# Prompt scores of the second query block: one plain fp32 product, or three fp32r products of high and low parts

## The chip, the cores and the metric

The kernel runs on one core of one Trainium2 chip. The metric is the device time of one execution in microseconds (us), taken as the median of several runs. The engines are named as in the profile: PE is TensorE, DVE is VectorE, ACT is ScalarE, POOL is GpSimd and SP is SyncE, which only issues transfers here. PEld is the weight load of PE.

## The reference, cut to what matters

The program computes one inference step of a decoder with two layers, for one prompt of 256 tokens and 8 sampled tokens: first a gated short convolution, then block-sparse attention with 8 heads of 128. The change lies in the prompt's attention. Since the prompt is exactly one attention block long, each head is plain causal attention over 256 positions:

```
s_own = jnp.einsum('bqhd,bkhd->bhqk', q, k_own, preferred_element_type=jnp.float32) * scale
own_ok = own_pos[None, :] <= q_pos[:, None]
s_own = jnp.where(own_ok[None, None], s_own, -jnp.inf)
...
p = jax.nn.softmax(jnp.concatenate([s_sel, s_own], axis=-1), axis=-1).astype(vs.dtype)
```

All inputs and outputs are fp32.

## The kernel before, in words

The kernel is a pipeline over slabs of weights. A slab is 1024 x 128 of a weight matrix; it is loaded by SP as `raw` (a 128x1024 tile), ACT rounds it into an fp32r tile `hi` (line 124), and DVE subtracts to get the remainder `lo` as another fp32r tile (line 129). The activations are split the same way: `pair[0]` and `pair[1]` each hold a high and a low tile (called m0h, m0l and m1h, m1l in the profile), with 8 rows of columns per partition. A product of fp32 accuracy is then three fp32r matmuls per 128 rows of the contraction: high by high, low by high, high by low (lines 136 to 138). That is 24 matmuls of 264 columns a slab (256 prompt tokens and 8 sampled ones).

Time is cut into slots, one for each slab n, written out by hand: `at(n, phase, f)` hangs a piece of work on slot n, and `begin(n)` runs the pieces phase after phase ("dma", "pe", "s0", "hi", "lo", "s1a", "s1b", "s1", "s1c"). Then come the first 12 matmuls of the slab, the phases "peh" and "s2", and the last 12 matmuls. Each engine works through its own instructions in exactly the order in which this program text issues them. The attention layer begins at slab S = 40. Slabs 47 and on read `pair[1]`, so `pair[0]` is unused from there until the gated attention output is written to it (line 802, from slot 65 on).

For head h the attention work is placed as follows, with n = 56 + h:

- slot n, "pe": `s_mm(h)` (line 646) computes the scores on PE. Query rows 0 to 127 against keys 0 to 127 is line 648, query rows 128 to 255 against all 256 keys is line 649. Both are plain fp32; each is one instruction in the program and two matmul records in the trace.
- slot n, "s0": `s_max(h)` on DVE adds the causal mask (line 657) and takes the two row maxima (659, 660). The slab's `hi` on ACT and `lo` on DVE come next.
- slot n, "s1b": `s_exp(h)` on ACT (line 666), then `s_norm(h)` on DVE (lines 671 to 673).
- slot n + 1, "peh": PE transposes the probabilities (`p_tr`, line 679) and the values (`v_tr`, 638); ACT copies both out in "s2" (683, 642).
- slot n + 2, "pe": the product with the values, `pv(h)` (lines 688, 689), right behind `s_mm(h + 2)`.

Some slots hold extra work on DVE. In slot 56, between its `lo` and `s_norm(0)`, stand the rotation of the sampled keys and their own score (lines 616 to 618 and 725). In slot 57, phase "s1c", stands the rotation of the keys of heads 4 to 7 (`rope`, lines 603 to 606). In slot 58, `d_max` (lines 732, 733) and then `d_norm` (740 to 742) belong to the sampled tokens. Slot 60 begins with a transpose for the sampled tokens (`pd_tr`, lines 749, 750), slot 62 with 32 matmuls of 512 columns (`pvd`, line 768).

Of the kernel before, what the change touches and what calls it, by code (L numbers as in the profile page):

```python
# [10 lines left out]
F32 = mybir.dt.float32  # L11
# [38 lines left out]
def build(tc, a):  # L50
    nc = tc.nc
    pe, act, dve, pool, sp = nc.tensor, nc.scalar, nc.vector, nc.gpsimd, nc.sync

    with ExitStack() as top:
# [13 lines left out]
        def att_tile(nm):  # L68
            return psp.tile([128, 512], F32, tag="att", bufs=3, name=nm)
# [7 lines left out]
        def keep_warm(n):  # L77
            wt = big_tile("warmp")
            for _ in range(n):
# [13 lines left out]
        pair = [[cp.tile([128, NB, ROW], F32R, name=f"m{i}{c}")[:, :, 4:N + 6] for c in "hl"]  # L93
                for i in range(2)]
# [48 lines left out]
        def at(n, phase, f, *args):  # L143
            hooks.setdefault((n, phase), []).append(lambda: f(*args))
# [383 lines left out]
        with tc.tile_pool(name="l1", bufs=1) as p1, ExitStack() as late_pool:  # L528
# [5 lines left out]
            qh = [p1.tile([128, N], F32, name=f"q{h}") for h in range(8)]  # L534
            kall = p1.tile([128, 8 * N], F32, name="kall")
            kh = [kall[:, N * h:N * h + N] for h in range(8)]
# [106 lines left out]

            P_t, PT_t, s_ps, pt_ps, o_ps = {}, {}, {}, {}, {}

            def s_mm(h):
                s = s_ps[h] = att_tile("s")
                pe.matmul(s[:, 0:128], qh[h][:, 0:128], kh[h][:, 0:128], start=True, stop=True)
                pe.matmul(s[:, 128:384], qh[h][:, 128:256], kh[h][:, 0:256], start=True, stop=True)  # L649

            AB = (np.s_[:, 0:128], np.s_[:, 128:384])
            mx_t = {}
# [201 lines left out]

            for h in range(8):
                n = S + 16 + h
                at(n, "pe", s_mm, h)
                at(n, "s0", s_max, h)
                at(n, "s1b", s_exp, h)
                at(n, "s1b", s_norm, h)  # L860
                at(n + 1, "peh", p_tr, h)
                at(n + 1, "peh", v_tr, h)
                at(n + 1, "s2", p_cp, h)
                at(n + 1, "s2", v_cp, h)

                at(n + 2, "s1a", o_cp, h)
# [136 lines left out]
            for i in range(2, 32):  # L1003
                n = S + i
# [11 lines left out]
                h = i % 8  # L1016
# [20 lines left out]
            r = rows[0]  # L1037
# [11 lines left out]
            r = rows[1]  # L1049
# [9 lines left out]
            for k in range(8):  # L1059
                for c in range(2):  # L1060
                    for j in range(4):
                        pe.matmul(ps[32 * j:32 * j + 32], gs[:, c, k, :],  # L1062
                                  wide(raws, k)[:, 256 * j + 128 * c:256 * j + 128 * c + 128],
                                  start=k == 0 and c == 0, stop=k == 7 and c == 1)
# [99 lines left out]
```

## Time and profile before

| what | value |
|---|---|
| median of 3 runs | 280.36 us (280.11 to 280.7) |
| the profiled execution's own time | 280.45 us |
| its span in the trace | 278.7 us |
| mean granted PE clock | 0.996 of full |
| busy: PE, PEld, DVE, ACT, POOL | 272.7, 255.6, 195.6, 155.3, 59.8 us |
| matmuls, moved bytes | 2330, 66.34 MB |

The span runs from the first to the last instruction of the trace; the time around it is 280.45 - 278.7 = 1.75 us. In a line of the trace the first number is the start in us from the start of the span and the second the duration of what is merged in that line; "xN" counts the instructions in it, and a bracket at the end says how long the engine had been idle before and who released it. Matmuls are pipelined: each is shown for some 0.28 us, but the next starts about 0.12 us after it, so that starts are compared, not durations.

### The profile page before, as it was taken

The numbers are of one execution on the slowest core, as the hardware profiler recorded it, in microseconds if no ns is written. First come the engines' busy times: TensorE is split into PE (matmuls) and PEld (weight loads), VectorE is DVE, ScalarE is ACT, GpSimd is POOL, SyncE is SP. The second block draws the span as 40 slices with busy tenths as digits, with TensorE's granted clock in tenths as the row PEclk, the third lists the DMA queues.
The fourth block names the chain that finished last, engine by engine and source line by source line (L and its number), as shares of the span: only waits on it lengthen the run. The fifth ranks groups of instructions, "written<-read, shape, count | busy, mean of one in ns | idle before, by whom it ended". The sixth has DMA issues, their size and how long they took to land.

```text
span 278.7 us, 6245 instructions
## 1 busy us (share of the span) xinstructions
PE 272.7 (98%) x2330; PEld 255.6 (92%) x2330; DVE 195.6 (70%) x377; ACT 155.3 (56%) x294; POOL 59.8 (21%) x130
## 2 busy tenths in 40 slices
PE   8999999999999999999999999999999999999992
PEld 5999999999999999999998997999959987988891
DVE  3868976655766768969999498498626384993745
ACT  4876564444655538557776495567746752571101
POOL 2110532020101102850311158411100030000212
PEclk9999999999999999999999999999999999999998
DMA  7985989999666876134025999999864995781012
GB/s 230 410 266 189 310 274 331 385 373 356 230 211 224 295 238 221 43 119 152 2 75 194 387 399 348 359 335 304 277 223 149 311 379 173 236 290 61 0 78 85
DMA packets 24495, 66.34 MB, mean 238 GB/s; under 512 B 3090, under 2 KB 6930, under 8 KB 24466
## 3 DMA queue, kind: packets, MB, share of 16 engines
q1 hardware_dynamic: 24178, 65.63, 67.4%
q8 instruction: 18, 0.29, 0.4%
q10 hardware_dynamic: 288, 0.33, 0.4%
q14 instruction: 11, 0.09, 0.1%
HBM read 61.55 MB, written 3.35 MB: 233 GB/s over the span
## 4 chain that ended last, share of the span: by engine, by line
PE 98%; DVE 1%; issue 0%
PE acc L136 24%; PE acc L138 24%; PE acc L137 24%; PE c L961 4%; PE sd L716 3%; PE dps L768 3%; PE acc L961 2%; PE acc L465 2%; PE acc L466 2%; PE acc L469 1%; PE so L1062 1%; PE warmp L80 1%; PE s L649 1%; PE o L688 1%; PE c1b L961 1%; PE c1c L961 1%
## 5 line engine op out<-in xcount | busy, mean ns | idle before, releaser
L124 ACT CAST hi<-raw 128x1024 fp32r<-128x1024 f32 x76 | 79.2, 1049 | 35.2 <-DMA raw<-w 22.1
L129 DVE TENSOR_TENSOR lo<-raw,hi 128x1024 fp32r<-128x1024 f32 x76 | 92.7, 1230 | 7.6 <-ACT hi L124 7.4
L138 PE MATMUL acc<-m0h,lo 128*128 128x264 f32 (+1 forms) x280 | 79.4, 284 | 0.0
L137 PE MATMUL acc<-m0l,hi 128*128 128x264 f32 (+1 forms) x280 | 79.3, 283 | 0.0
L136 PE MATMUL acc<-m0h,hi 128*128 128x264 f32 (+1 forms) x280 | 79.3, 283 | 0.0
L136 PE MATMUL acc<-m1h,hi 128*128 128x264 f32 x264 | 76.6, 290 | 0.0
L138 PE MATMUL acc<-m1h,lo 128*128 128x264 f32 x264 | 74.8, 283 | 0.0
L137 PE MATMUL acc<-m1l,hi 128*128 128x264 f32 x264 | 74.7, 283 | 0.0
L136 PEld LDWEIGHTS acc<-m0h,hi 128*128 128x128 f32 x280 | 52.7, 188 | 0.2
L138 PEld LDWEIGHTS acc<-m0h,lo 128*128 128x128 f32 x280 | 52.8, 189 | 0.0
L137 PEld LDWEIGHTS acc<-m0l,hi 128*128 128x128 f32 x280 | 52.7, 188 | 0.0
L136 PEld LDWEIGHTS acc<-m1h,hi 128*128 128x128 f32 x264 | 49.7, 188 | 1.7 <-issue 1.7
L137 PEld LDWEIGHTS acc<-m1l,hi 128*128 128x128 f32 x264 | 49.7, 188 | 0.1
L138 PEld LDWEIGHTS acc<-m1h,lo 128*128 128x128 f32 x264 | 49.7, 188 | 0.0
L421 POOL COPY uo<-up 128x10 f32<-128x10 f32 x8 | 8.0, 1002 | 66.8 <-DVE up L420 58.9
L657 DVE TENSOR_TENSOR s<-s,cst 128x256 f32<-128x256 f32 x8 | 3.4, 430 | 14.7 <-PE s L649 14.7
L799 DVE TENSOR_TENSOR gt<-z,q 128x256 f32<-128x256 f32 x8 | 3.4, 423 | 9.4 <-ACT z L796 9.4
L932 ACT ACTIVATE row<-row,epst 128x1 f32<-128x1 f32 x2 | 0.6, 295 | 16.6 <-DVE row L931 16.6
L666 ACT ACTIVATE P<-s,mx 128x128 f32<-128x128 f32 (+1 forms) x16 | 6.6, 416 | 5.6 <-DVE mx L660 5.6
L796 ACT ACTIVATE z<-acc 128x264 f32<-128x264 f32 x8 | 3.1, 391 | 11.4 <-PE acc L138 11.4
L628 POOL COPY vs<-vh 128x8 f32<-128x8 f32 x8 | 1.6, 204 | 34.9 <-ACT vh L627 34.9
L466 PE MATMUL acc<-m0l,hi 128*128 128x264 f32 x32 | 8.9, 306 | 0.0
(215 smaller groups left out, 415.4 us busy)
## 6 DMA issues: line engine op xcount, KB each, us to landing
raw<-w SPq DMA_DIRECT2D x76, 512.0 KB, 4.7
kv<-kc SPq DMA_DIRECT2D x32, 256.0 KB, 5.7
kv<-vc SPq DMA_DIRECT2D x16, 512.0 KB, 6.6
first<-first SPq DMA_DIRECT2D x6, 388.0 KB, 6.9
k_o<-kall SPq DMA_DIRECT2D x8, 132.0 KB, 5.1
v_o<-vh SPq DMA_DIRECT2D x8, 132.0 KB, 5.2
xf<-kall SPq DMA_DIRECT2D x16, 64.0 KB, 3.1
kall<-gb SPq DMA_DIRECT2D x2, 512.0 KB, 5.0
```

What stands on the lines that cost most here:

```text
L124: act.copy(his[n][sl], raws[n][sl])
L129: dve.tensor_sub(los[n][sl], raws[n][sl], his[n].bitcast(F32)[sl])
L136: pe.matmul(acc, wh, mh[:, k, 0:w], start=first and k == ks[0], stop=False)
L137: pe.matmul(acc, wh, ml[:, k, 0:w], start=False, stop=False)
L138: pe.matmul(acc, wl, mh[:, k, 0:w], start=False, stop=last and k == ks[-1])
L421: pool.tensor_copy(uo[:, f], up[:, T:N + 2])
L465: pe.matmul(accs[s], wh, mh, start=k == 0, stop=False)
L466: pe.matmul(accs[s], wh, ml, start=False, stop=False)
L666: act.activation(P[sl], s_ps[h][sl], AF.Exp, bias=mx[:, 2 + i:3 + i], scale=SCALE, accum_out=mx[:, 4 + i:5 + i])
L716: pe.matmul(s[32 * j:32 * j + 16, 0:256], zq[:, o:o + 16], kt, start=step == 0 and i == 0, stop=step == 3 and i == 3)
L768: pe.matmul(dps[0][32 * j:32 * j + 32, 512 * c:512 * c + 512], pm[b2][pg][:, j, :], kv_tiles[step, j][:, 512 * c:512 * c + 512], start=ste ...
L961: pe.matmul(acc, g[m][:, k, t], wide(d, k)[:, c0:c1], start=k == 0 and i == 0, stop=k == 7 and i == 2)
```

## The change

`s_mm(h)` keeps the first product (query rows 0 to 127) as it is. The second one becomes three fp32r matmuls of 256 columns that accumulate in the same place: query high by key high, query high by key low, query low by key high. A new function `qk_split(h)` makes the parts: ACT casts the 256 key columns and the 128 query columns to fp32r (two instructions), and DVE subtracts each from its fp32 source (two instructions). The parts are kept in `pair[0]`, in the two rows 2 (h mod 4) and the next. `qk_split(h)` hangs on slot 55 + h, phase "s1c": one slot ahead of its `s_mm(h)`, behind everything else that `begin` issues in that slot.

```
+            def qk_part(h, c):
+                r = 2 * (h % 4)
+                return pair[0][c][:, r, 0:256], pair[0][c][:, r + 1, 0:128]
+
+            def qk_split(h):
+                src = kh[h][:, 0:256], qh[h][:, 128:256]
+                for d, x in zip(qk_part(h, 0), src):
+                    act.copy(d, x)
+                for d, x, y in zip(qk_part(h, 1), src, qk_part(h, 0)):
+                    dve.tensor_sub(d, x, y.bitcast(F32))
+
             def s_mm(h):
                 s = s_ps[h] = att_tile("s")
                 pe.matmul(s[:, 0:128], qh[h][:, 0:128], kh[h][:, 0:128], start=True, stop=True)
-                pe.matmul(s[:, 128:384], qh[h][:, 128:256], kh[h][:, 0:256], start=True, stop=True)
+                for i, (c, d) in enumerate(((0, 0), (0, 1), (1, 0))):
+                    pe.matmul(s[:, 128:384], qk_part(h, c)[1], qk_part(h, d)[0], start=i == 0, stop=i == 2)
...
             for h in range(8):
                 n = S + 16 + h
+                at(n - 1, "s1c", qk_split, h)
                 at(n, "pe", s_mm, h)
```

Lines behind this place are numbered 12 to 13 higher in the changed kernel (657 becomes 669, 673 becomes 685). The changed scores are line 661 there, the casts line 653, the subtractions line 655.

The order of DVE in slot 56, from its `lo` to the mask of head 1, is this before:

```order
L129 TENSOR_TENSOR lo_2692<-raw_2486,hi_2643 128x1024
L616 STREAM_SHUFFLE qsr<-ks 32x64
L617 TENSOR_SCALAR ks<-ks,cst 32x64
L618 SCALAR_TENSOR_TENSOR ks<-qsr,cst,ks 32x64
L725 TENSOR_TENSOR pr<-qs,ks 128x4x8 x2
L671 RECIPROCAL mx<-mx 128x2
L673 TENSOR_SCALAR P<-P,mx 128x128
L673 TENSOR_SCALAR P<-P,mx 128x256
L657 TENSOR_TENSOR s<-s,cst 128x2x128
```

and with the change this (m0h and m0l are the two tiles of `pair[0]`):

```order
L129 TENSOR_TENSOR lo_2698<-raw_2486,hi_2643 128x1024
L616 STREAM_SHUFFLE qsr<-ks 32x64
L617 TENSOR_SCALAR ks<-ks,cst 32x64
L618 SCALAR_TENSOR_TENSOR ks<-qsr,cst,ks 32x64
L737 TENSOR_TENSOR pr<-qs,ks 128x4x8 x2
L683 RECIPROCAL mx<-mx 128x2
L685 TENSOR_SCALAR P<-P,mx 128x128
L685 TENSOR_SCALAR P<-P,mx 128x256
L655 TENSOR_TENSOR m0l<-kall,m0h 128x256
L655 TENSOR_TENSOR m0l<-q_1856,m0h 128x128
L669 TENSOR_TENSOR s<-s,cst 128x2x128
```

The two subtractions of head 1 stand behind the normalisation of head 0 and ahead of the mask of head 1.

The order of DVE in slot 57, from the normalisation of head 1 to the mask of head 2, is this before:

```order
L671 RECIPROCAL mx<-mx 128x2
L673 TENSOR_SCALAR P<-P,mx 128x128
L673 TENSOR_SCALAR P<-P,mx 128x256
L603 STREAM_SHUFFLE rsh<-rp 128x264
L604 TENSOR_TENSOR rp<-rp,cst 128x264
L605 TENSOR_TENSOR rsh<-rsh,cst 128x264
L606 TENSOR_TENSOR rp<-rp,rsh 128x264
L657 TENSOR_TENSOR s<-s,cst 128x2x128
```

and with the change this:

```order
L683 RECIPROCAL mx<-mx 128x2
L685 TENSOR_SCALAR P<-P,mx 128x128
L685 TENSOR_SCALAR P<-P,mx 128x256
L603 STREAM_SHUFFLE rsh<-rp 128x264
L604 TENSOR_TENSOR rp<-rp,cst 128x264
L605 TENSOR_TENSOR rsh<-rsh,cst 128x264
L606 TENSOR_TENSOR rp<-rp,rsh 128x264
L655 TENSOR_TENSOR m0l<-kall,m0h 128x256
L655 TENSOR_TENSOR m0l<-q_1857,m0h 128x128
L669 TENSOR_TENSOR s<-s,cst 128x2x128
```

The subtractions of head 2 stand behind the whole rotation.

On PE, the start of slot 57 (scores of head 1, then the slab's matmuls) is this before:

```order
L648 MATMUL s<-kall,q_1856 128x128
L649 MATMUL s<-kall,q_1856 128x256
L136 MATMUL acc<-m1h,hi_2482 128x264
L137 MATMUL acc<-m1l,hi_2482 128x264
L138 MATMUL acc<-m1h,lo_2533 128x264
```

and with the change this:

```order
L659 MATMUL s<-kall,q_1856 128x128
L661 MATMUL s<-m0h 128x256
L661 MATMUL s<-m0l,m0h 128x256
L661 MATMUL s<-m0h,m0l 128x256
L136 MATMUL acc<-m1h,hi_2482 128x264
L137 MATMUL acc<-m1l,hi_2482 128x264
L138 MATMUL acc<-m1h,lo_2533 128x264
```

The second of the three takes the low part of the keys, the third the low part of the queries, and the slab's matmuls stand behind them.

## The prediction

> **What bounds the kernel now.** First the page: its busy line and the chain of work that ended last. Then the list of PE's waits, complete.
>
> ```profile
> PE 272.7 (98%) x2330; PEld 255.6 (92%) x2330; DVE 195.6 (70%) x377; ACT 155.3 (56%) x294; POOL 59.8 (21%) x130
> ...
> PE 98%; DVE 1%; issue 0%
> ```
> ```profile
> PE st L1079 <- DVE row L1076: 1.2, 1, 1.2
> PE warmp L80 <- PEq L1145: 0.8, 1, 0.8
> ```
>
> PE is the path from end to end, and waits only at the very start and the very end, 2.0 us in all. So any PE time saved in the middle shortens the run, and any new wait of PE lengthens it by its full length, because no later slack on PE could absorb it. Two questions decide: what do the products cost on PE, and are the new operands there when PE reaches them?
>
> For the second I read the timeline of PE and of DVE over slots 56 to 61. PE first: the starts of the scores of heads 0 to 5 and of what follows.
>
> ```profile
> 177.51 0.60 PE L649 MATMUL s<-kall,q 128*128 128x256 f32 x2
> ...
> 180.84 0.38 PE L648 MATMUL s<-kall,q 128*128 128x128 f32 x2
> 181.06 0.60 PE L649 MATMUL s<-kall,q 128*128 128x256 f32 x2
> ...
> 181.61 0.28 PE L137 MATMUL acc<-m1l,hi 128*128 128x264 f32 x1
> ...
> 185.07 0.47 PE L648 MATMUL s<-kall,q 128*128 128x128 f32 x2
> 185.37 0.60 PE L649 MATMUL s<-kall,q 128*128 128x256 f32 x2
> 185.81 0.59 PE L688 MATMUL o<-PT,vt 128*128 128x256 f32 x2
> ...
> 189.91 0.38 PE L648 MATMUL s<-kall,q 128*128 128x128 f32 x2
> ...
> 195.32 0.60 PE L649 MATMUL s<-kall,q 128*128 128x256 f32 x2
> ...
> 199.85 0.38 PE L648 MATMUL s<-kall,q 128*128 128x128 f32 x2
> ```
>
> Then DVE in the same stretch.
>
> ```profile
> 178.14 0.43 DVE L657 TENSOR_TENSOR s<-s,cst 128x256 f32<-128x256 f32 x1 [5.01 <-PE s L649]
> ...
> 179.47 1.21 DVE L129 TENSOR_TENSOR lo<-raw,hi 128x1024 fp32r<-128x1024 f32 x1
> ...
> 180.62 0.21 DVE L616 STREAM_SHUFFLE qsr<-ks 32x64 f32<-32x64 f32 x1
> ...
> 181.92 0.55 DVE L673 TENSOR_SCALAR P<-P,mx 128x128 f32<-128x128 f32 x2
> 182.38 0.42 DVE L657 TENSOR_TENSOR s<-s,cst 128x256 f32<-128x256 f32 x1
> ...
> 185.37 0.45 DVE L603 STREAM_SHUFFLE rsh<-rp 128x264 f32<-128x264 f32 x1
> ...
> 187.02 0.42 DVE L657 TENSOR_TENSOR s<-s,cst 128x256 f32<-128x256 f32 x1
> ...
> 190.01 0.42 DVE L732 TENSOR_REDUCE dst<-sd 128x1 f32<-128x257 f32 x1
> 190.46 0.15 DVE L733 TENSOR_SCALAR dst<-dst 128x1 f32<-128x1 f32 x1
> ...
> 196.03 0.43 DVE L657 TENSOR_TENSOR s<-s,cst 128x256 f32<-128x256 f32 x1 [0.91 <-PE s L649]
> ...
> 198.56 0.55 DVE L673 TENSOR_SCALAR P<-P,mx 128x128 f32<-128x128 f32 x2
> ```
>
> What to see: DVE idles 5.01 us ahead of head 0's mask, and then falls behind. PE issues the scores of head 1 at 181.06 and of head 2 at 185.37; DVE masks them only at 182.38 and 187.02. That lag costs nothing today, since PE needs the outcome half a slot later. With the change DVE's work becomes an input of the scores themselves.
>
> **What the change saves on PE.** From line 649 to line 688 behind it lie 185.81 - 185.37 = 0.44 us. In slot 57, line 137 starts at 181.61, one matmul of 0.12 behind line 136, so line 649 held PE for 181.49 - 181.06 = 0.43. The nearest row for an fp32r matmul of 256 columns is the last projection, whose 128x256 matmuls run back to back; here are the first and the 16th of 24.
>
> ```profile
> 263.58 0.28 PE L961 MATMUL c1b<-hi,m0h 128*128 128x256 f32 x1
> ...
> 265.34 0.28 PE L961 MATMUL c1b<-hi,m0h 128*128 128x256 f32 x1
> ```
>
> That is 1.76 / 15 = 0.117 us each, 0.35 for three. Saved are 0.435 - 0.352 = 0.083 us a head, 0.66 us for 8 heads. The Trainium skill (TensorE: Matmul & The Clock Gate, Back-to-back issue gap) gives N / 2.4 + 2.5 ns between warm matmuls, an estimate of 109 ns at 256 columns and so of 0.87 us saved. The row says 117 ns with a weight load for each matmul, and I take the row.
>
> **What it adds on ACT and DVE.** The nearest rows are the same split of the gated output: a cast and a subtraction of 128x256. For 128x128 I take 0.29, a vector instruction of that size.
>
> ```profile
> L802 ACT CAST m0h<-gt 128x256 fp32r<-128x256 f32 x8 | 3.3, 407 | 2.4 <-DVE gt L799 2.4
> ```
> ```profile
> L803 DVE TENSOR_TENSOR m0l<-gt,m0h 128x256 fp32r<-128x256 f32 x8 | 3.2, 401 | 0.0
> ...
> L742 DVE TENSOR_SCALAR dg<-cst,pd 128x128 f32<-128x128 f32 x1 | 0.3, 290 | 0.0
> ```
>
> The next instruction starts some 0.05 before the end of the one ahead (182.38 against 181.92 + 0.55 = 182.47 above), so the low part of the keys is there 0.40 us after DVE turns to it and that of the queries after 0.65. A release from DVE to PE takes 0.06, by the one place where PE waited for DVE (274.21 against 273.75 + 0.40):
>
> ```profile
> 273.75 0.40 DVE L1076 TENSOR_TENSOR row<-g,row 128x48 f32<-128x48 f32 x1
> ```
> ```profile
> 274.21 0.42 PE L1079 MATMUL st<-row,g 128*128 128x48 f32 x2 [1.18 <-DVE row L1076]
> ```
>
> **Are the parts there in time? Slot by slot.** I give the shift of PE against before.
>
> Head 0: ACT ends its `hi` of slot 55 at 175.92, DVE has nothing to do.
>
> ```profile
> 174.87 1.05 ACT L124 CAST hi<-raw 128x1024 fp32r<-128x1024 f32 x1
> ...
> 180.31 0.20 ACT L666 ACTIVATION_READ_ACCUMULATOR P<-s,mx 128x1 f32 x1
> ```
>
> Two casts (0.8 at most) and the subtractions (0.65) end by 177.4, ahead of 177.51: no wait, shift -0.08.
>
> Head 1, slot 57: ACT is through with `s_exp(0)` at 180.51, so its casts are done by 181.3. DVE is not. Up to the end of `s_norm(0)` its order is unchanged, and the subtractions start where head 1's mask started, at 182.38 - 0.08 = 182.30. The queries' low part lands at 182.95, PE can start the third product at 183.01. Without waiting it would have started it at 180.98 (181.06 - 0.08) + 2 x 0.117 = 181.21. **Wait 1.80 us.** Behind it in PE's queue stand all 24 matmuls of slab 57, which need none of this. Shift: -0.08 + 1.80 - 0.08 = +1.64.
>
> Head 2, slot 58: the mask of head 1 can start 0.31 after the third product's start (its 0.28 and a release): 183.32 instead of 182.38. From there to the end of `rope` DVE runs without a gap: 187.02 - 182.38 = 4.64 us. Subtractions from 187.96, third product at 187.96 + 0.65 + 0.06 = 188.67. PE would be ready for it at 185.37 + 1.64 + 0.23 (the first two products) = 187.24. **Wait 1.43 us.** Behind it stand `pv(0)` and slab 58. Shift: 1.64 + 1.43 - 0.08 = +2.99.
>
> Head 3, slot 59: mask of head 2 at 188.98; up to `d_max` 190.01 - 187.02 = 2.99, `d_max` 0.60, subtractions 0.65: 193.22, release 193.28. PE would be ready at 189.91 + 2.99 + 0.22 (line 648's product, 181.06 - 180.84) + 0.23 = 193.35. No wait, with 0.07 to spare.
>
> Heads 4 to 7: the extra work on DVE is over and `pv` fills PE. From mask to the end of `s_norm` DVE takes 3.0 (196.03 to 199.02, `d_max` excluded), so from one third product to the readiness of the next 0.31 + 3.0 + 0.71 = 4.0. PE takes from one to the next 199.85 - 195.32 + 0.22 = 4.75, less the 0.08 saved. Some 0.6 us to spare; slot 62's matmuls add more.
>
> **The sum** against the profiled execution's 280.45: + 1.80 + 1.43 - 0.66 = +2.57, so 283.0 us. That execution lies 0.09 over the median of 280.36, which changes nothing.
>
> One cost the trace hardly shows: the third product's stationary operand is the part waited for, so its weight load cannot run ahead. Line 1079 is such a case, with no gap to be seen; a whole load of 0.19 us is the upper bound.
>
> ```profile
> L136 PEld LDWEIGHTS acc<-m1h,hi 128*128 128x128 f32 x264 | 49.7, 188 | 1.7 <-issue 1.7
> ```
>
> I take 0; twice 0.19 would give 283.4. A gain is excluded, since a load can't end before its data.
>
> **Rivals.**
> - *The parts come in time.* PE then keeps its pace and only the saving is left: 280.45 - 0.66 = 279.8, faster. For it: DVE is 70% busy, and idle 5.01 us just ahead. It decides if the subtractions of head 1 land by 181.15, which is 1.8 us earlier than I find; the order puts 2.9 us of `lo`, key rotation and `s_norm` (179.47 to 182.38) ahead of them, and these durations hardly vary. Chance 6%.
> - *Every later slot waits too.* Head 3 has 0.07 us to spare, heads 4, 5 and 7 some 0.6. If DVE or ACT lose 0.4 more a slot, by the casts that now stand ahead of the copies of lines 683 and 642 on ACT, then slots 57 to 59 grow by 0.4 each: 284.2. Chance 12%.
> - *The clock falls.* The granted clock is 1.00 through a PE wait of 1.18 us, but fell some 1.8 us after the last matmul:
>
> ```profile
> 272.90:274.20 1.30, 0.14 (x8) 0.00 (x0) 1.03 (x4) 0.00 (x0) 1.11 (x2) 1.00 0.54 202
> 274.20:276.40 2.20, 0.42 (x2) 0.30 (x2) 1.57 (x5) 0.29 (x1) 0.00 (x0) 1.00 0.32 119
> 276.40:277.00 0.60, 0.00 (x0) 0.00 (x0) 0.00 (x0) 0.00 (x0) 0.00 (x0) 0.53 0.24 74
> ```
>
>   PE had been busy 0.56 of the 3.5 us before that; beside my waits it is busy over half of any such stretch, which speaks against it. At the start of the run a matmul took 5.63 - 5.42 = 0.21 instead of 0.12:
>
> ```profile
> 5.42 0.42 PE L466 MATMUL acc<-m0l,hi 128*128 128x264 f32 x1
> 5.63 0.42 PE L465 MATMUL acc<-m0h,hi 128*128 128x264 f32 x1
> ```
>
>   A stretch of 3.5 us at that pace loses 1.5 us, so 284.5 for one fall. The Trainium skill (TensorE: Matmul & The Clock Gate, The HAM clock gate) has the clock halve only after an idle window of about 3.4 us; by that rule waits of 1.8 and 1.4 us leave it alone, and the 1.18 us wait agrees. Chance 5%.
> - *Only the first wait is real.* 280.45 + 1.80 - 0.66 = 281.6. The second falls away only if DVE makes up the rotation's 1.65 us (185.37 to 187.02). Chance 4%.
>
> **How the numbers follow.** My forecast keeps 73%: 283.0. From 281.4 (only one wait, and that a little shorter) to 284.7 (every slot, or one fall of the clock) all but the first rival is covered, as are the bounds of the weight load. A difference under 0.2%, 0.56 us, is about what a measurement of this kernel cannot tell from none. Only the first rival is faster, and by 0.66 us barely over that: faster 5%, within 0.2% 3%, slower 92%.
>
> **What would show it.** In the changed profile PE's waits list gets two entries of the new score products behind DVE's subtractions, about 1.8 and 1.4 us, in slots 57 and 58; none in 56 and from 60 on. The three products take 0.35 us where nothing waits, and the slab's matmuls keep 0.12. DVE's mask of head 1 starts near 183.3. The granted clock stays at 1.00. I am wrong if PE waits nowhere, if the waits recur in every slot, or if PE makes up the lost time behind slot 59.

## The result and the profile after

The changed kernel takes 283.37 us, the kernel before 280.24 us beside it (medians of six runs each). One of the six runs of the changed kernel took 731.17 us; without it the median is 283.28 us, and the ratio leaves it out. The ratio is 1.0105, with a 95% interval of 1.0086 to 1.0125: slower by about 3 us (2.4 to 3.5), where 283.0 us was forecast. The profiled execution took 283.79 us, with a span of 282.0 us and a mean granted clock of 0.995.

The busy line and the chain of the changed kernel's page:

```profile
PE 273.2 (97%) x2338; PEld 255.4 (91%) x2338; DVE 201.1 (71%) x393; ACT 158.6 (56%) x310; POOL 61.7 (22%) x130
...
PE 92%; DVE 4%; DMA 2%; ACT 0%; issue 0%; SPq 0%
```

PE's busy time has hardly moved, but DVE now holds 4% of the chain. The chain also follows DVE's own work back from a wait, so its 4% is more than the waits alone. (Busy times of pipelined matmuls overlap, so the saving on PE can't be read from them.) The first row of the list of PE's waits names the place; the columns are the total, the number of waits and the longest:

```profile
PE s L661 <- DVE m0l L655: 2.6, 2, 1.4
```

Line 661 is the three products, line 655 DVE's subtractions: two waits that were not there before. The rows behind it are at the start and the end of the run, as before; one of them, 0.2 us at 8.73 us from the start, is not in the list of the kernel before, and lies ahead of everything compared below. The timeline of PE shows where the two are, with the scores of heads 0 to 3 (slots 56 to 59) and the second block of value products of the sampled tokens as a mark behind the change:

```profile
177.54 0.38 PE L659 MATMUL s<-kall,q 128*128 128x128 f32 x2
...
181.01 0.38 PE L659 MATMUL s<-kall,q 128*128 128x128 f32 x2
181.31 0.39 PE L661 MATMUL s<-m0h 128*128 128x256 f32 x1
183.10 0.38 PE L661 MATMUL s<-m0l,m0h 128*128 128x256 f32 x1 [1.40 <-DVE m0l L655]
183.32 0.36 PE L661 MATMUL s<-m0h,m0l 128*128 128x256 f32 x1
183.52 0.28 PE L136 MATMUL acc<-m1h,hi 128*128 128x264 f32 x1
...
187.10 0.47 PE L659 MATMUL s<-kall,q 128*128 128x128 f32 x2
187.33 0.36 PE L661 MATMUL s<-m0h 128*128 128x256 f32 x1
188.85 0.39 PE L661 MATMUL s<-m0l,m0h 128*128 128x256 f32 x1 [1.16 <-DVE m0l L655]
189.25 0.39 PE L661 MATMUL s<-m0h,m0l 128*128 128x256 f32 x1
189.48 0.59 PE L700 MATMUL o<-PT,vt 128*128 128x256 f32 x2
...
193.60 0.38 PE L659 MATMUL s<-kall,q 128*128 128x128 f32 x2
193.74 0.36 PE L661 MATMUL s<-m0h 128*128 128x256 f32 x1
...
194.18 0.60 PE L700 MATMUL o<-PT,vt 128*128 128x256 f32 x2
...
231.93 3.64 PE L780 MATMUL dps<-kv,pm 128*32 128x512 f32 x32
```

And three of these places in the kernel before: the first score product, the product with the values in slot 59, and the mark behind the change.

```profile
177.29 0.38 PE L648 MATMUL s<-kall,q 128*128 128x128 f32 x2
...
190.56 0.59 PE L688 MATMUL o<-PT,vt 128*128 128x256 f32 x2
...
228.60 3.64 PE L768 MATMUL dps<-kv,pm 128*32 128x512 f32 x32
```

From the first score product to that last mark are 51.31 us before and 54.39 us after: +3.08 us. I call this the stretch below. It is steadier than the span, since runs differ by some tenths before they come to slot 56 at all (177.29 and 177.54 here).

Head 3 waits for nothing: its scores take 194.18 - 193.60 = 0.58 us, where 190.56 - 189.91 = 0.65 were needed before, so a head saves 0.07. Had head 1 run like that, slab 57's matmuls would have begun at 181.01 + 0.58 = 181.59; they began at 183.52, a loss of 1.93. Head 2 takes 0.66 where it does not wait (the experiment with the rotation moved, below, has 186.90 to 187.56), so it lost 189.48 - 187.76 = 1.72. Together 1.93 + 1.72 - 8 x 0.07 = 3.09, all of the stretch's 3.08. (Where nothing waits, the three products by themselves take 194.18 - 193.74 = 0.44 us from start to start, no less than line 649 did; the 0.07 shows ahead of them, where line 661 starts 0.14 behind line 659 and line 649 started 0.22 behind line 648.)

DVE of the changed kernel, around these two places:

```profile
182.62 0.42 DVE L655 TENSOR_TENSOR m0l<-kall,m0h 128x256 fp32r<-128x256 f32 x1
182.96 0.29 DVE L655 TENSOR_TENSOR m0l<-q,m0h 128x128 fp32r<-128x128 f32 x1
...
188.37 0.42 DVE L655 TENSOR_TENSOR m0l<-kall,m0h 128x256 fp32r<-128x256 f32 x1
188.71 0.49 DVE L655 TENSOR_TENSOR m0l<-q,m0h 128x128 fp32r<-128x128 f32 x1
```

Both third products start 0.05 to 0.07 after the end of the second subtraction (183.32 behind 183.25, 189.25 behind 189.20). The granted clock held through both waits. These are the two waits as stretches of the view by window (busy us of PE, PEld, DVE, ACT, POOL, then the granted clock, the DMA share and GB/s):

```profile
181.31:183.10 1.79, 0.39 (x3) 0.19 (x2) 1.68 (x9) 1.22 (x2) 0.26 (x1) 1.00 1.06 407
...
187.33:188.85 1.52, 0.36 (x4) 0.17 (x3) 1.49 (x5) 1.16 (x2) 0.76 (x2) 1.00 0.82 232
```

### The profile page after: what moved, and what is told of

Same layout as the page of the kernel before. It is cut to its first block, busy times and chain, and to the rows that moved or that the text cites. A ratio compares the mean times of both kernels' runs of the same rounds, so it can differ in the third digit from the quotient of the medians.

```text
span 282.0 us, 6286 instructions
## 1 busy us (share of the span) xinstructions
PE 273.2 (97%) x2338; PEld 255.4 (91%) x2338; DVE 201.1 (71%) x393; ACT 158.6 (56%) x310; POOL 61.7 (22%) x130
## 4 chain that ended last, share of the span: by engine, by line
PE 92%; DVE 4%; DMA 2%; ACT 0%; issue 0%; SPq 0%
PE acc L136 23%; PE acc L138 23%; PE acc L137 23%; PE c L974 4%; PE sd L728 3%; PE dps L780 3%; DMA first<-first 2%; PE acc L974 2%; PE so L1075 1%; PE s L661 1%; PE o L700 1%; PE acc L465 1%; PE acc L466 1%; PE acc L469 1%; PE c1b L974 1%; PE c1c L974 1%
## 5 line engine op out<-in xcount | busy, mean ns | idle before, releaser
L421 POOL COPY uo<-up 128x10 f32<-128x10 f32 x8 | 9.0, 1122 | 65.5 <-DVE up L420 59.6
L465 PE MATMUL acc<-m0h,hi 128*128 128x264 f32 x32 | 8.9, 306 | 0.3 <-ACT hi L215 0.2
```

The costliest lines, as they stand in the source:

```text
L421: pool.tensor_copy(uo[:, f], up[:, T:N + 2])
L465: pe.matmul(accs[s], wh, mh, start=k == 0, stop=False)
```

## The experiments

My theory was that the whole loss is PE standing at the head of its queue for DVE's subtractions in slots 57 and 58, that the split costs nothing where PE does not wait for it, and that the three products by themselves save 0.66 us. The rivals: the added casts and subtractions cost time wherever they stand; the products save nothing; DVE bounds every slot. Times are compared with the kernel before in the same session (279.97 us for the first four runs of the table behind the change, 280.21 for the next four).

| run | time, us | ratio to before (95%) | stretch, us |
|---|---|---|---|
| kernel before | 279.97 to 280.24 | 1 | 51.31 |
| the change | 283.37 | 1.0105 (1.0086 to 1.0125) | 54.39 |
| heads 0 to 3 split early | 280.29 | 1.0008 (0.9996 to 1.0019) | 51.35 |
| split, not used | 281.85 | 1.0074 (1.0059 to 1.0088) | 52.96 |
| products alone | 279.93 | 0.9999 (0.9987 to 1.0010) | 50.86 |
| rotation behind the split | 282.68 | 1.0098 (1.0080 to 1.0115) | 53.54 |
| early, and ahead of the exponentials | 279.60 | 0.9981 (0.9968 to 0.9993) | 50.86 |
| casts alone | 280.60 | 1.0003 (0.9990 to 1.0017) | 51.65 |
| subtractions alone | 281.39 | 1.0046 (1.0029 to 1.0064) | 52.46 |
| subtractions twice | 284.95 | 1.0168 (1.0155 to 1.0181) | 55.96 |
| POOL's copy later | one run | - | 54.16 |

**Heads 0 to 3 split early.**

```
-                at(n - 1, "s1c", qk_split, h)
+                at(n - 1 if h > 3 else S + 14 + h // 2, "s1c", qk_split, h)
```

> Only the place of the split changes for heads 0 to 3: heads 0 and 1 are split in slot 54, heads 2 and 3 in slot 55, where DVE stood idle for 5.0 us before. Heads 4 to 7 stay where they are. Theory (PE loses time only where it reaches a product before DVE's subtraction, in slots 57 and 58): both waits go, and only the cheaper products are left, so 0.66 us below the kernel before, 279.6 us if that reads 280.2. Rival (the added casts and subtractions cost time wherever they stand): it stays slower than the kernel before, between 281 and 283.4 us.

The waits for DVE are gone, and with them the 3 us: 1.0008. But the saving did not appear. The trace shows one new wait, in slot 60, on PE and on ACT:

```profile
195.03 0.39 PE L762 MATMUL pdt<-dg,onesf 128*128 128x128 f32 x2
195.67 0.46 PE L659 MATMUL s<-kall,q 128*128 128x128 f32 x2 [0.25 <-ACT PT L695]
```
```profile
194.45 0.20 ACT L678 ACTIVATION_READ_ACCUMULATOR P<-s,mx 128x1 f32 x1
194.55 0.40 ACT L653 CAST m0h<-kall 128x256 fp32r<-128x256 f32 x1
...
195.04 0.48 ACT L695 COPY PT<-pt 128x384 f32<-128x384 f32 x1
```

The scores of head 4 came 0.64 us after line 762, where the changed kernel takes 0.23: they waited for ACT to copy the transposed probabilities (line 695) out of PSUM. Between the exponentials, which end at 194.65, and that copy now stand head 4's two casts.

**The split made, but not used.**

```
-                for i, (c, d) in enumerate(((0, 0), (0, 1), (1, 0))):
-                    pe.matmul(s[:, 128:384], qk_part(h, c)[1], qk_part(h, d)[0], start=i == 0, stop=i == 2)
+                pe.matmul(s[:, 128:384], qh[h][:, 128:256], kh[h][:, 0:256], start=True, stop=True)
```

> The split of all heads is made as in the change, but the scores are computed by the plain fp32 product, so that nobody reads the parts. Theory (the split is harmless as long as PE does not wait for it): DVE's mask starts up to 0.6 us later, which PE does not feel, so within 0.3 us of the kernel before, 280.2 us; PE has no wait in slots 56 to 63. Rival (DVE's or ACT's load by itself delays the pipeline): 281 us or more.

The theory failed here: 1.0074, 2.1 us slower, though no product reads the parts. The row of its PE waits that is new in these slots, and the start of slot 58:

```profile
PE o L699 <- ACT vt L642: 0.4, 2, 0.2
```
```profile
185.10 0.60 PE L660 MATMUL s<-kall,q 128*128 128x256 f32 x2
185.91 0.70 PE L699 MATMUL o<-PT,vt 128*128 128x256 f32 x2 [0.21 <-ACT vt L642]
```

The product with the values starts 0.81 us after the scores here and 0.80 in slot 59, where it took 0.44 and 0.43 before, because ACT's copy of the transposed values is late. That is some 0.74 of the 1.65 us by which the stretch grew. The first score product is late too, by 0.19 us in slot 58, 0.13 in slot 59 and 0.17 in slot 60 (measured from the matmul ahead of it, against the kernel before). Both halves of the split push that copy back: DVE's subtractions delay the mask and so the exponentials, and ACT's casts stand behind these. In the changed kernel this is hidden, since PE is held up for longer by the products themselves: there the copy ends at 187.11, and the product with the values follows at 189.48.

**The products alone.** The split is dropped, and the products read rows that are ready long before, so the scores of query rows 128 to 255 are left out.

```
-                return pair[0][c][:, r, 0:256], pair[0][c][:, r + 1, 0:128]
+                return pair[1][c][:, r, 0:256], pair[1][c][:, r + 1, 0:128]
...
-                at(n - 1, "s1c", qk_split, h)
```

> The three fp32r products are kept but read rows of the activations that have long been split, and nothing is split for them (the scores of query rows 128 to 255 are left out, so the output is not the attention's). It measures the PE term alone. Theory: 0.083 us less for each of 8 heads, 0.66 us below the kernel before, 279.6 us. Rival (switching between plain fp32 and fp32r products costs PE something): no gain, 280.2 us or more.

The stretch is 0.45 us shorter than before; the time is level, and its interval reaches from 0.36 us faster to 0.28 slower. Both are short of 0.66. By these runs alone neither side is shown.

**The rotation behind the split of head 2.**

```
-                at(n - 1, "s1c", qk_split, h)
+                at(n - 1, "s1" if h == 2 else "s1c", qk_split, h)
```

> As the change, but in slot 57 the split of head 2 stands ahead of the keys' rotation instead of behind it; all else is the same. Theory (the second wait is the rotation's 1.65 us on DVE ahead of the subtractions): the wait in slot 58 falls from some 1.4 us to under 0.2, the one in slot 57 stays, so 1.3 to 1.7 us below the changed kernel, about 281.8 us. Rival (DVE is simply behind, whatever stands ahead): no more than 0.5 us below the changed kernel, about 283 us.

```profile
186.90 0.47 PE L659 MATMUL s<-kall,q 128*128 128x128 f32 x2
...
187.56 0.59 PE L700 MATMUL o<-PT,vt 128*128 128x256 f32 x2
...
191.82 0.36 PE L661 MATMUL s<-m0h 128*128 128x256 f32 x1
192.69 0.38 PE L661 MATMUL s<-m0l,m0h 128*128 128x256 f32 x1 [0.51 <-DVE m0l L655]
...
193.12 0.59 PE L700 MATMUL o<-PT,vt 128*128 128x256 f32 x2
```

Slot 58 has no wait any more, as the theory had it, but slot 59 has one: from line 661 to line 700 are 1.30 us where 0.44 are needed (193.74 to 194.18 in the changed kernel). The stretch shrank by 0.85 us, not by 1.3 to 1.7; by the times it is 0.2 us, with an interval that includes the 0.85. The expectation missed because I moved DVE's arrears instead of removing them: the rotation's 1.65 us came ahead of the next mask, and head 3 had only about 0.2 us to spare.

**Early, and heads 4 to 7 ahead of the exponentials.**

```
-                at(n - 1, "s1c", qk_split, h)
+                at(*((n - 1, "s1a") if h > 3 else (S + 14 + h // 2, "s1c")), qk_split, h)
```

> As the run in which heads 0 to 3 are split in slots 54 and 55, and beside it heads 4 to 7 are split in phase s1a of the same slot as in the change: on ACT ahead of the exponentials instead of behind them, so that the casts no longer stand ahead of the copies of the transposed probabilities and values. Theory (what ate the saving there was PE waiting 0.4 us in slot 60 for a PSUM bank that one of these copies gives back): that wait goes, and only the cheaper products are left: 0.4 to 0.6 us below the kernel before, 279.4 to 279.6 us if that reads 280.0. Rival (the saving is given back elsewhere, as the run with the products alone suggests, which was level with the kernel before): within 0.2 us of the kernel before.

```profile
192.36 0.42 ACT L653 CAST m0h<-kall 128x256 fp32r<-128x256 f32 x1
...
193.19 0.37 ACT L678 ACTIVATE P<-s,mx 128x128 f32<-128x128 f32 x1 [0.21 <-DVE mx L672]
...
193.90 0.20 ACT L678 ACTIVATION_READ_ACCUMULATOR P<-s,mx 128x1 f32 x1
194.00 0.48 ACT L695 COPY PT<-pt 128x384 f32<-128x384 f32 x1
```
```profile
194.48 0.39 PE L762 MATMUL pdt<-dg,onesf 128*128 128x128 f32 x2
194.70 0.39 PE L659 MATMUL s<-kall,q 128*128 128x128 f32 x2
```

As expected: 0.9981 (0.9968 to 0.9993), 0.5 us faster than the kernel before, and the fastest run here. The casts fill time in which ACT waited for DVE's mask, so the copy of line 695 follows the exponentials at once, and the wait of slot 60 is gone. The operations are those of the change, one by one; only their places differ.

One new wait of 0.15 us is left, in slot 59, where PE now comes earlier. The transposes of the values (line 638) load their weights only when ACT has ended its copy of the product with the values (line 704, 192.48):

```profile
192.10 0.38 ACT L704 COPY q<-o 128x256 f32<-128x256 f32 x1
```
```profile
192.53 0.20 PEld L638 LDWEIGHTS vtp<-cst,vh 128*128 128x128 f32 x2 [0.17 <-ACT q L704]
```

**Casts alone, subtractions alone.** Both with the plain product; each leaves out one loop of `qk_split`.

```
-                for d, x, y in zip(qk_part(h, 1), src, qk_part(h, 0)):
-                    dve.tensor_sub(d, x, y.bitcast(F32))
```

> Only ACT's two casts a head are added at the place of the change; there are no subtractions, and the scores are the plain fp32 product. Theory (ACT's copies of the transposed probabilities and values, which follow the casts, have some 0.55 to 0.8 us to spare before PE needs them, and the casts take 0.6): a PE wait of 0 to 0.1 us in one or two slots, so 0 to 0.3 us above the kernel before. Rival (the casts alone make up the run with the whole split and no use of it): 1.5 to 2 us above.

```
-                for d, x in zip(qk_part(h, 0), src):
-                    act.copy(d, x)
```

> Only DVE's two subtractions a head are added at the place of the change (they read rows that hold other data); there are no casts, and the scores are the plain fp32 product. Theory (each 0.65 us puts DVE's mask, so the exponentials, so ACT's copies that much further behind in slots 57 and 58, where DVE never idles): waits of the product with the values in slots 59 and 60, 0.5 to 1.0 us above the kernel before; with the casts alone less than the 1.9 us of both, since the spare time is used up only once. Rival (DVE's share is nothing): within 0.2 us of the kernel before.

The casts alone are level with the kernel before (1.0003; the stretch is 0.34 us longer), as expected. The subtractions alone cost 1.3 us (1.0046, so 0.8 to 1.8; the stretch is 1.15 longer), near the 0.5 to 1.0 expected, but not at the place expected: the product with the values waits nowhere, and starts 0.43 us after the scores in slots 58 and 59 as before. What is late is the first score product, by 0.18 us in slot 58 and 0.61 in slot 59. This is slot 59, with the end of ACT's exponentials of head 2 and the weight load of the scores of head 3:

```profile
189.94 0.20 ACT L675 ACTIVATION_READ_ACCUMULATOR P<-s,mx 128x1 f32 x1
```
```profile
190.20 0.30 PEld L657 LDWEIGHTS s<-kall,q 128*128 128x128 f32 x2 [0.63 <-issue]
```

The load starts 0.06 us after the exponentials of the head before are through (190.14). In slot 58 it is the same, 184.75 behind 184.69, and with the split made but not used 184.78 behind 184.71 and 190.22 behind 190.16. The profile names no releaser here. The times fit a wait for the PSUM bank of the scores of the head before, which the exponentials read last; in the program all tiles of this stage share three banks. If so, DVE's subtractions delay the mask, that delays the exponentials, and these delay the next scores.

DVE's share is the larger one. The two alone add up to 1.4 us by the times and 1.49 by the stretch, both at once to 2.1 and 1.65. Whether the two add up or make each other worse is within the intervals, and not shown.

**Subtractions twice.**

```
-                for d, x, y in zip(qk_part(h, 1), src, qk_part(h, 0)):
-                    dve.tensor_sub(d, x, y.bitcast(F32))
+                for _ in range(2):
+                    for d, x, y in zip(qk_part(h, 1), src, qk_part(h, 0)):
+                        dve.tensor_sub(d, x, y.bitcast(F32))
```

> As the change, but DVE makes both subtractions of each head twice, 0.62 us more a head. Theory (DVE's work ahead of the product is what PE waits for, in slots 57 and 58, with 0.2 us to spare in slot 59 and 0.6 to 0.8 from 60 on): the waits grow by 0.62, 0.62 and 0.4 us in slots 57, 58 and 59, so 1.5 to 1.9 us above the changed kernel, about 285 us. Rival (DVE bounds every slot): 8 times 0.62, 5 us above it, 288 us; the other rival (PE waits for ACT's casts): no change.

```profile
PE s L662 <- DVE m0l L656: 3.8, 2, 1.9
```

284.95 us, 1.6 us over the changed kernel by the medians, and a stretch longer by 1.57: as expected for three slots that wait and five that do not. The third, slot 59, is too short for the list; there the scores take 195.14 - 194.09 = 1.05 us instead of 0.58. Eight slots would have made 5 us.

**POOL's copy later.**

```
-                at(S + (13, 13, 14, 14, 18, 19, 20, 21)[h], "s1", rows_back, 1, h)
+                at(S + (13, 13, 14, 14, 19, 19, 20, 21)[h], "s1", rows_back, 1, h)
...
-                at(S + (15 if h < 4 else 19) + h % 4, "dma", k_store, h)
+                at(S + (15 if h < 4 else 20) + h % 4, "dma", k_store, h)
```

> As the change, but POOL's copy of the rotated rows into the keys of head 4 is moved from slot 58 to slot 59 (and that head's store a slot later), so that POOL no longer writes while DVE makes the second subtraction of head 2. Theory (that subtraction took 0.49 instead of 0.28 us in the changed kernel because POOL copied beside it): it takes 0.28 to 0.30 us, the third product of head 2 starts 0.2 us sooner, and the stretch from the first score product to the second block of value products of the sampled tokens is 0.2 us shorter than 54.4 us. Rival (its length has to do with what stands ahead of it on DVE): still 0.49 us. The total time of a single run says nothing here.

In the changed kernel POOL copied beside the subtraction that took 0.49 us:

```profile
188.52 0.53 POOL L611 COPY kall<-rp 32x264 f32<-32x264 f32 x1 [0.48 <-DVE rp L606]
```

With the copy moved, DVE and PE at the same place:

```profile
188.65 0.42 DVE L655 TENSOR_TENSOR m0l<-kall,m0h 128x256 fp32r<-128x256 f32 x1
188.99 0.28 DVE L655 TENSOR_TENSOR m0l<-q,m0h 128x128 fp32r<-128x128 f32 x1
```
```profile
189.12 0.38 PE L661 MATMUL s<-m0l,m0h 128*128 128x256 f32 x1 [1.16 <-DVE m0l L655]
189.34 0.37 PE L661 MATMUL s<-m0h,m0l 128*128 128x256 f32 x1
```

The subtraction takes 0.28 us, the third product follows the second after 0.22 instead of 0.40, and the stretch is 0.23 shorter. As expected.

## Why the prediction was right, point by point

- **Direction, place and mechanism** held: two waits of PE for DVE's subtractions, in slots 57 and 58, none from 59 on, and PE makes up nothing behind them. The doubled subtractions and the early split show it from both sides. The size was near, but all three terms of the sum erred the same way: +2.57 us was forecast, and the stretch grew by 3.08.
- **The wait in slot 57** was put at 1.80 us and was a loss of 1.93. DVE came to the subtractions at 182.62, which is 182.37 without the 0.25 us that this execution was late from the start, against 182.30. Most of the rest is the weight load: I took 0 for it. Behind the waiting product the next matmul starts 0.20 us later instead of 0.12 (183.32 to 183.52), so 0.08 more, inside the bound of 0.19 that I gave. The two subtractions were put at 0.65 us and took 0.63 (182.62 to 183.25): in the line that I quoted the next instruction starts 0.09 us before the end of the one ahead, not 0.05.
- **The wait in slot 58** was put at 1.43 us and was a loss of 1.72. Of the 0.29 missing, 0.2 is the second subtraction, which took 0.49 us and not 0.29 beside POOL's copy, and 0.11 the weight load (189.25 to 189.48 against 0.12). This is the term of the sum that was mis-sized most.
- **The saving** was put at 0.083 us a head and was 0.07 where nothing waits; over 8 heads 0.56, not 0.66. The sign that I named for it, three products in 0.35 us, did not come: they take 0.44, and the saving shows ahead of the first of them. Without waits for the split, the stretch was shorter by 0.45 in two different runs; in both, slot 60 began 0.12 to 0.15 us later behind the transposes of slot 59 than before, where PE now comes too early for ACT. The transposes of the values wait there for ACT's copy of line 704, as the run "early, and ahead of the exponentials" shows above; with the products alone the same two rows are at 191.74 and 192.17, the same distance. By the times, one of these was level with the kernel before and the other 0.5 us faster; their intervals share 0.2 to 0.36 us. The estimate by the Trainium skill (TensorE: Matmul & The Clock Gate, Back-to-back issue gap), 0.87 us in the prediction (0.86 by its own terms), is further off than the row that I took.
- **Slots 60 to 63** had time to spare, as forecast: in the changed kernel there is no wait there.
- **What the prediction missed** is that the split has a cost of its own even where its result is not waited for, 2.1 us, by way of ACT: its copies for the product with the values come late, and so do the exponentials, behind which the next scores start. I named the casts ahead of these copies as a rival and thought of it as added to the forecast. In the changed kernel the two don't add up: a PE that is held up 1.9 us at the scores comes to the values late enough for ACT. The total was right partly for that reason, which is luck. A cost of the same kind, the casts ahead of ACT's copy in slot 60, is what a first attempt to remove the waits ran into.
- **The clock** did not fall: 1.00 through both waits, which were listed at 1.40 and 1.16 us, and 1.00 through one listed at 1.94 us in the run with the subtractions twice. That agrees with the Trainium skill (TensorE: Matmul & The Clock Gate, The HAM clock gate), whose idle window is about 3.4 us. The price that I gave for a fall, 1.5 us, rests on a pace of 0.21 us a matmul at the start of the run; the profile lists a granted clock of 1.00 there too (5.42 to 6.51 us), so the lower clock is not shown to be the cause of that pace, and the price stays untested.

Open is by how much the products alone shorten the time: 0.45 us in the trace, between 0.2 and 0.4 us where the intervals of the two runs meet. Also open is whether the late first score product in the run with the subtractions alone waited for a PSUM bank: the times fit it in four places, but the profile names no releaser.

## What to carry to other kernels

When PE is the path from end to end, the price of an operand made on another engine is not its busy share but that engine's arrears at the place where PE arrives: follow the engine's own order from its last idle moment, and add up. Moving work ahead of or behind other work on an engine in arrears only hands the wait to the next slot; moving it to where the engine idles (here, for the two heads that waited, two slots earlier, and for the later heads on ACT into the time in which it waits for DVE) removes it. Here that turned the same operations from 1.05% slower into 0.2% faster.

## What the runs showed of the hardware

- A subtraction of 128x128 on DVE with both sources in SBUF took 0.49 us beside a POOL copy of 32x264, and 0.28 without. The change and the runs with the split not used, the subtractions alone and the subtractions twice all show the 0.49 beside a POOL copy of 0.53 at this place; the 0.28 there is one run, that with the copy later. The Trainium skill (SBUF — State Buffer, SBUF: two separate sides) says that a DVE operation with two SBUF inputs and a GpSimd operation that reads SBUF exclude each other on a shared pair of ports, the later one waiting for the end of the first. The end of the subtraction at 189.20, 0.15 us after the copy's at 189.05, fits a wait, though one shorter than a full start behind the copy, which would have ended at 189.33.
- A matmul whose weights were waited for costs the one behind it: 0.20 and 0.23 us from start to start instead of 0.12. Of 1.93 and 1.72 us lost the list of waits shows 1.40 and 1.16, so here the list understates what a stop of PE cost. In slot 57 some 0.16 of the difference lies ahead of the listed wait: line 661 first starts 0.30 us behind line 659 instead of 0.14, 0.06 after ACT ended the cast of head 1's queries (181.25).
